# Modulating gathered tokens on their way out of PSUM, a projection in token-tile order, and small tables behind the first expert chunks

## The chip, the cores and the metric

The kernel runs on one core of a Trainium2 chip. The metric is the device time of one execution, in microseconds (us); smaller is better. Of several executions the median is taken.

## The reference, cut to what matters

One layer: a token mixer, a LayerNorm, and a mixture of experts in which each of 256 tokens goes to 4 of 32 experts. `sc2` and `sh2` are rows made from the conditioning vector; what the change touches lies between the mixer's last product and the experts' first.

```python
h = _layer_norm(x) * (1 + sc1) + sh1
y = _token_mixer(h, ...)              # ends with  m @ w_out + b_out
x = _layer_norm(ALPHA * x + g1 * y, post1_g, post1_b)
h = _layer_norm(x) * (1 + sc2) + sh2  # "second modulation"
logits = h @ w_router + b_router      # 256 x 32
top_logits, top_idx = lax.top_k(logits, 4)
top_w = jax.nn.softmax(top_logits)
for each expert e, over its tokens:   # 32 experts
    gate, up = split(h[tok] @ w_gu[e] + b_gu[e])     # 1024 x 2048 weights
    act = (min(gate, 7) * sigmoid(1.702 * gate)) * (clip(up, -7, 7) + 1)
    y[tok] += top_w * (act @ w_dn[e] + b_dn[e])      # 1024 x 1024 weights
x = _layer_norm(ALPHA * x + g2 * y, post2_g, post2_b)
```

Everything is float32, D is 1024, and the 256 tokens are two tiles of 128 (t = 0 and 1).

## The kernel before

**The mixer** takes the first 300 us or so. Its products are made of pieces: a float32 operand is split in a high and a low part (ACT casts the high one, DVE subtracts for the low one, L148 for weights, L119 for activations), and three matmuls make one product. Some weight chunks are "native", that is, used unsplit.

**The chain** leads from the mixer to the experts. The projection with `w_out` (L685 to L705) takes four chunks of 1 MB; chunk 0 is native and the other three are split. Its loop goes over pairs of chunks, in each over the two token tiles, and calls `prepare()` and `prepare_router()` in the middle of it. For each tile the LayerNorm follows on DVE (`c_mul` L739, `c_add` L745 and L747, `c_gain` L758, `c_norm` L761; squares and roots on ACT), giving `hn`, the normalised and not yet modulated tokens. `hn` is transposed on PE (L768), multiplied with the router's weights, into which `prepare_router()` has folded the modulation (L778), and `c_top` (L792 on) finds the four experts. In parallel `c_h2` puts the second modulation on `hn` with two POOL operations (L781, L782) and splits the result `h2` for the gather. Ranks of the experts, places of the tokens and one-hot matrices follow. `g2_step` sets single matmuls of another product (`g2`, L493) between all this as filling.

**The gather** (`gather`, `gather_mm` L944) multiplies one-hot matrices with `h2_hi` and `h2_lo` and leaves the tokens of a batch of jobs in columns of a PSUM tile, four groups (kk = 0 to 3) of two 128-row blocks each; ACT copies each group to SBUF (L968).

**The experts' stream**: 30 jobs, the first for expert 0 (its weights can be loaded before the router has run) and 29 for experts chosen by their rank in number of tokens, each with a fixed capacity of 192, 128, 64 or 32 tokens. The first has 64. A job takes 8 chunks of gate/up weights (`gu_mm`, L1095 and L1106) and 4 chunks of down weights (L1237, L1246), 1 MB each, in two rings of 7 and 4 buffers that SP fills (L197, L205). Small pieces of other jobs are "units": lists of steps that `begin()` and `tick()` run one at a time between chunks, from the list `waiting`. Tokens beyond an expert's capacity are taken by tail jobs; the tables that these need and the bias columns of all jobs are made once, after the first gather and before the first chunk (L1003 to L1049), and the combine weights right behind (`c_exp`, `c_comb`, transposes L1325). The four "start units" (L1313) begin the output with the down bias.

**What sets the order.** Each engine works its instructions in the order in which they stand in its queue. DVE's order is as written from L724 to the end; PE's and ACT's is as written till `chain.close()`, and a scheduler's after it. Where the scheduler chooses, as in the mixer, an edit can move instructions that it doesn't name.

## Time and profile before

| | us |
|---|---|
| median of 3 runs | 1285.02 (1281.32 to 1288.55) |
| the profiled execution | 1284.86 |
| its span | 1282.8 |
| PE busy | 1132.3 (88%) |
| DVE busy | 489.0 (38%) |
| ACT busy | 195.0 (15%) |
| POOL busy | 65.2 (5%) |
| moved by DMA | 449.12 MB, mean 350 GB/s |
| PE's granted clock, mean | 0.946 of full |

The span begins with the first instruction and ends with the last; 2.06 us of the execution's time lie outside of it. The busy share is a mean over stages that differ: in the mixer DVE and PE are both full, in the chain no engine is, and in the stream the DMA moves some 415 GB/s for most of the time. All times below are from the start of the span.

### The profile page before, as it was taken

The page shows a single profiled execution, that of the slowest core. Times are in us where ns is not written, and L with a number is a line of the kernel's source. Part 1 is how long each engine was busy: PE and PEld are TensorE (multiplying, and loading weights), DVE is VectorE, ACT ScalarE, POOL GpSimd, SP SyncE. Part 2 cuts the span into 40 slices and gives each one's busy share as a digit, 9 for nine tenths or more (in the row PEclk, how much of TensorE's full clock was granted, in tenths as well). Part 3 has the DMA queues.
Part 4 walks back from the last instruction along what each step waited for, and adds up shares of the span by engine and source line. Part 5 has one row for each costly group of instructions (what it writes and reads, how often), then busy time and mean ns, then how long its engine had stood idle before and what let it go on. Part 6 is the DMA issues. An engine that isn't in the chain of part 4 may idle for free. (4 is left out here: it accounts for less than half of the span.)

```text
span 1282.8 us, 14332 instructions
## 1 busy us (share of the span) xinstructions
PE 1132.3 (88%) x5454; PEld 553.7 (43%) x5454; DVE 489.0 (38%) x921; ACT 195.0 (15%) x316; POOL 65.2 (5%) x189
## 2 busy tenths in 40 slices
PE   1999999997999989999997999899888977998772
PEld 1998898875534324324331343234222321333110
DVE  6799999867411320321321203222121211132113
ACT  1533233443011000100110010011000100010000
POOL 6000000002300001000010010000000000000000
PEclk9999999998899999999998999899889988899676
DMA  9983446775499999899999999999999999999992
GB/s 366 371 319 132 131 135 208 269 272 227 166 403 388 392 368 387 327 393 402 380 417 417 417 416 401 409 416 416 416 417 416 417 418 417 417 416 417 417 413 77
DMA packets 84311, 449.12 MB, mean 350 GB/s; under 512 B 7377, under 2 KB 7417, under 8 KB 51424
## 3 DMA queue, kind: packets, MB, share of 16 engines
q1 hardware_dynamic: 82672, 443.84, 86.7%
q0 software_dynamic: 1552, 4.15, 0.9%
q8 instruction: 50, 0.82, 0.3%
q14 instruction: 37, 0.30, 0.1%
HBM read 446.92 MB, written 1.05 MB: 349 GB/s over the span
## 5 line engine op out<-in xcount | busy, mean ns | idle before, releaser
L1095 PE MATMUL big<-raw,S 128*32 128x512 f32 (+1 forms) x1600 | 280.3, 632 | 35.4 <-DMA raw<-in_w_gu_dram 35.4
L1106 PE MATMUL big<-raw,S 128*128 128x512 f32 x384 | 175.3, 610 | 0.0
L1271 DVE TENSOR_TENSOR ob<-big,g2c 64x512 f32<-64x512 f32 x48 | 33.1, 689 | 362.9 <-PE big L1246 255.2
L1095 PEld LDWEIGHTS big<-raw,S 128*32 128x32 f32 (+1 forms) x1600 | 63.1, 122 | 210.4 <-issue 129.0
L1106 PEld LDWEIGHTS big<-raw,S 128*128 128x128 f32 x384 | 72.9, 195 | 92.7 <-issue 92.4
L517 DVE SCALAR_TENSOR_TENSOR sg<-ya,par,sg 128x256 f32<-128x256 f32 x240 | 100.3, 476 | 0.7
L1246 PE MATMUL big<-raw,aT 128*32 128x512 f32 x512 | 74.9, 699 | 27.0 <-DMA raw<-in_w_dn_dram 25.7
L1237 PE MATMUL big<-raw,aT 128*128 128x512 f32 x192 | 86.9, 600 | 0.0
L427 PE MATMUL big<-hT,raw 128*128 128x256 f32 x384 | 85.5, 379 | 0.0
L1299 PE MATMUL ms<-ob,ohT 128*128 128x512 f32 x144 | 77.0, 647 | 5.2 <-DVE gt L1139 3.2
L1291 DVE TENSOR_TENSOR y<-y,ms 128x512 f32<-128x512 f32 x72 | 49.0, 686 | 80.7 <-PE ms L1299 80.6
L427 PEld LDWEIGHTS big<-hT,raw 128*128 128x128 f32 x384 | 71.8, 190 | 9.6 <-issue 0.5
L1095 PE MATMUL big<-raw,aT 128*64 128x512 f32 x256 | 63.3, 611 | 4.9 <-DMA raw<-in_w_dn_dram 4.9
L148 DVE TENSOR_TENSOR lo<-raw,hi 128x1024 fp32r<-128x1024 f32 x46 | 55.2, 1217 | 5.9 <-ACT hi L147 4.3
L1237 PEld LDWEIGHTS big<-raw,aT 128*128 128x128 f32 x192 | 35.2, 190 | 51.2 <-issue 51.2
L431 PE MATMUL big<-hThi,lo 128*128 128x256 f32 x192 | 55.1, 289 | 0.8 <-DVE lo L148 0.8
L429 PE MATMUL big<-hThi,hi 128*128 128x256 f32 x192 | 55.8, 291 | 0.0
L147 ACT CAST hi<-raw 128x1024 fp32r<-128x1024 f32 x46 | 46.2, 1050 | 59.5 <-DMA raw<-in_w_in_dram 17.8
L430 PE MATMUL big<-hTlo,hi 128*128 128x256 f32 x192 | 55.0, 287 | 0.1
L1129 ACT COPY g<-big 128x512 f32<-128x512 f32 x16 | 9.4, 585 | 299.0 <-PE big L1095 299.0
L1139 DVE TENSOR_TENSOR gt<-ms,bcols 128x256 f32<-128x256 f32 (+1 forms) x46 | 22.6, 492 | 83.7 <-PE ms L1165 83.7
L1165 PE MATMUL ms<-ident,g 128*128 128x128 f32 x224 | 37.1, 296 | 15.7 <-ACT g L1129 7.6
(329 smaller groups left out, 1176.8 us busy)
## 6 DMA issues: line engine op xcount, KB each, us to landing
raw<-in_w_gu_dram SPq DMA_DIRECT2D x240, 1024.0 KB, 16.7
raw<-in_w_dn_dram SPq DMA_DIRECT2D x120, 1024.0 KB, 16.0
raw<-in_w_mod_dram SPq DMA_DIRECT2D x24, 1024.0 KB, 7.5
raw<-in_w_in_dram SPq DMA_DIRECT2D x24, 1024.0 KB, 6.7
raw<-in_w_b_dram SPq DMA_DIRECT2D x4, 1024.0 KB, 4.9
raw<-in_w_a_dram SPq DMA_DIRECT2D x4, 1024.0 KB, 4.9
raw<-in_w_out_dram SPq DMA_DIRECT2D x4, 1024.0 KB, 7.8
x<-in_x_dram SPq DMA_DIRECT2D x1, 1024.0 KB, 8.7
```

Of the source, the lines that this page charges most:

```text
L148: ve.tensor_tensor(c.lo[q], src, f(c.hi[q]), op=ALU.subtract)
L427: pe.matmul(o, lhsT=ck.raw[:, k2 * D + n * P:k2 * D + (n + 1) * P], rhs=af[:, k], start=b0, stop=b1)
L429: pe.matmul(o, lhsT=ck.hi[k2][:, s], rhs=ahi[:, k], start=b0, stop=False)
L430: pe.matmul(o, lhsT=ck.hi[k2][:, s], rhs=alo[:, k], start=False, stop=False)
L431: pe.matmul(o, lhsT=ck.lo[k2][:, s], rhs=ahi[:, k], start=False, stop=b1)
L517: ve.scalar_tensor_tensor(cT[:, n], ya[:, n, t:t + T], bcol(n, t), cT[:, n], op0=ALU.mult, op1=ALU.add)
L1095: pe.matmul(out_[q * n:(q + 1) * n], lhsT=S, rhs=raw[:, w0(q):w0(q) + 512], start=first_, stop=last_)
L1106: pe.matmul(job.ps[h][:, n * 512:(n + 1) * 512], lhsT=S[:, k, 0:P], rhs=raw[:, h * D + n * 512:h * D + (n + 1) * 512], start=f0, stop=f1)
L1237: pe.matmul(job.pd[0][:, n * 512:(n + 1) * 512], lhsT=job.aT[:, k, 0:P], rhs=raw[:, k2 * D + n * 512:k2 * D + (n + 1) * 512], start=f0, st ...
L1246: pe.matmul(job.pd[0][q * 32:(q + 1) * 32, 0:512], lhsT=job.aT[:, k, 0:32], rhs=raw[:, k2 * D + h * 512:k2 * D + (h + 1) * 512], start=ci ...
L1291: ve.tensor_tensor(yy, yy, box[0], op=ALU.add)
L1299: pe.matmul(box[0], lhsT=w()[r, t * P:(t + 1) * P], rhs=o(n)[r], start=i == 0, stop=i == len(parts_) - 1)
```

## The change

Five things are done. (1) The gather takes `hn` in place of `h2`, and the modulation is put on as a group of gathered tokens leaves PSUM, by two ACTIVATE operations on 128x256 with a scale and a bias column (`gather_out`) in place of one copy of 128x512; `h2` and its POOL operations are gone. (2) The projection does both tiles of the native chunk, then the rest of tile 0, then the rest of tile 1, and there by halves of the output (n). (3) The LayerNorm's sums are taken in halves with BN_STATS (`c_sum`, `c_first`), the router's weights are 32 columns wide and not 128, and the filling matmuls are dealt out otherwise (`G2`). (4) The first job's chunk 0 stands behind the first two groups of the gather, and groups 2 and 3 between later chunks. (5) Tail tables, bias columns, combine weights and the `g2` addition become units that run between the first job's chunks.

```diff
-N_RAW, N_HI, N_LO = 5, 9, 5
+N_RAW, N_HI, N_LO = 5, 9, 6
-H2_POOL = True
-G2 = (5, 1, 1, 1, 1, 1, 1)
+G2 = (4, 3, 2, 1, 1)
...
-        wr = rows.tile([P, KC, P], F32, name="wr", tag="row")
-        gp.memset(wr, 0.0)
+        wr = rows.tile([P, KC, E], F32, name="wr", tag="row")
...
+    pairs = [(ci, k2) for ci in range(4) for k2 in range(2)]
+    for t in range(NT):
+        for ci, k2 in pairs[:2]:
+            for n in range(2):
+                out_mm(t, ci, k2, n)
+    prepare()
+    for ci, k2 in pairs[2:]:
+        for n in range(2):
+            out_mm(0, ci, k2, n)
+    prepare_router()
+    for n in range(2):
+        for ci, k2 in pairs[2:]:
+            out_mm(1, ci, k2, n)
...
+    def c_sum(t, n):
+        ns = slice(n * 512, (n + 1) * 512)
+        if n == 0:
+            L[t]["b"] = sm.tile([P, 2, 6], F32, name=nm("cbst"), tag="cbst")
+        ve.tensor_tensor(hn[:, t, ns], yo[t][:, ns], g1[:, ns], op=ALU.mult)
+        ve.tensor_tensor(x1[:, t, ns], hn[:, t, ns], x1[:, t, ns], op=ALU.add)
+        ve.bn_stats(L[t]["b"][:, n], x1[:, t, ns])
+    def c_first(t):
+        mv = L[t]["mv"] = small("mv", 2)
+        ve.bn_aggr(mv, L[t]["b"])
+        L[t]["r", 0] = small("crs", bufs=4)
+        sc.activation(L[t]["r", 0], mv[:, 1:2], AF.Sqrt, bias=eps, scale=1.0)
+        ve.scalar_tensor_tensor(x1[:, t], x1[:, t], mv[:, 0:1], p1[:, 0], op0=ALU.subtract, op1=ALU.mult)
...
-    def c_h2(t, eng0, eng1):
-        eng0.tensor_tensor(h2[:, t], hn[:, t], sc2, op=ALU.mult)
-        eng1.tensor_tensor(h2[:, t], h2[:, t], sh2, op=ALU.add)
-        sc.copy(h2_hi[:, t], h2[:, t])
+    def c_hi(t):
+        sc.copy(hn_hi[:, t], hn[:, t])
...
+    c_second(0)
+    c_sum(1, 0)
+    c_rec(0, 1)
+    c_norm(0)
...
+    c_transpose(0)
+    c_copies(0)
+    c_hi(0)
+    g2_step(G2[0])
+    c_sum(1, 1)
+    c_first(1)
...
+    def gather_out(S, ps, kk, n):
+        for i in range(2):
+            k = kk * 2 + i
+            sc.activation(S[:, k, 0:n], ps[:, i * T:i * T + n], AF.Identity, bias=modc[:, 1, k:k + 1],
+                          scale=modc[:, 0, k:k + 1])
...
-                sc.copy(S[:, kk * 2:kk * 2 + 2, 0:n], box[0].rearrange("p (k s) -> p k s", k=2)[:, :, 0:n])
+                gather_out(S, box[0], kk, n)
...
-            waiting += start_units()
+            waiting += [tail_unit(), bias_unit(0), bias_unit(1), weight_unit(), gate_unit()] + start_units()
+            first_gather = gather(0)
...
+                if j == 0 and k % 2 == 0:
+                    first_gather[k // 2][1]()
+                    if k < KC - 2:
+                        first_gather[k // 2 + 1][0]()
                 tick()
                 gu_mm(job, k, raw)
                 next_gu()
                 begin()
```

`tail_unit`, `bias_unit` and `weight_unit` hold the operations of L1003 to L1049 and of the combine weights, cut into two or three steps each.

Three places show how instructions move. The first is DVE in the chain's LayerNorm, from the point at which the second tile's sums begin. `big_2314` in before and `big_2313` in after are the second tile's projection in PSUM, the first `hn` row writes the first tile's normalised tokens (in after `hn` also takes the product with g1). Before:

```order
L739 TENSOR_TENSOR h_226_2309<-big_2314,g_27_331 128x1024
L755 RECIPROCAL crs_2524<-crs_2524 128x1
L747 SCALAR_TENSOR_TENSOR x_227_2310,s_271_2530<-x_227_2310,crs_2524,pair_2354 128x1024
L748 TENSOR_SCALAR s_271_2530<-s_271_2530 128x1
L745 SCALAR_TENSOR_TENSOR x_227_2310,s_274_2537<-h_226_2309,x_227_2310 128x1024
L748 TENSOR_SCALAR s_274_2537<-s_274_2537 128x1
L755 RECIPROCAL crs_2535<-crs_2535 128x1
L761 TENSOR_SCALAR hn_2512<-x_227_2310,s_271_2530,crs_2535 128x1024
L758 SCALAR_TENSOR_TENSOR x_227_2310<-x_227_2310,s_274_2537,pair_2354 128x1024
```

After, with what each waits for (PE, ACT, DVE itself):

```order
L766 SCALAR_TENSOR_TENSOR x_226_2309,s_269_2529<-x_226_2309,crs_2525,pair_2335 128x1024 [waits DMASW3_49,DVE_49]
L767 TENSOR_SCALAR s_269_2529<-s_269_2529 128x1 [waits DVE_49]
L749 TENSOR_TENSOR hn_2510<-big_2313,g_27_331 128x512 [waits PE_49]
L750 TENSOR_TENSOR x_226_2309<-hn_2510,x_226_2309 128x512 [waits DVE_49]
L751 BN_STATS cbst_2536<-x_226_2309 128x6 [waits DVE_49]
L761 RECIPROCAL crs_2534<-crs_2534 128x1 [waits Activation_49]
L774 TENSOR_SCALAR hn_2510<-x_226_2309,s_269_2529,crs_2534 128x1024 [waits DVE_49]
L749 TENSOR_TENSOR hn_2510<-big_2313,g_27_331 128x512
L750 TENSOR_TENSOR x_226_2309<-hn_2510,x_226_2309 128x512 [waits DVE_49]
```

The first tile's second half of the LayerNorm (L747, now L766) moves ahead of the second tile's first operation, but the first tile's norm (L774) stays behind an operation of the second tile that waits for PE (L749), and of the second tile's two halves only the first one waits.

The second place is PE in the chain, from the end of the projection on; L493 (after: L492) are the filling matmuls, `ms<-ident,hn` the transposes of a tile, `big<-wr` the router. Before:

```order
L493 MATMUL big_2470<-raw_2471,condT 128x512 x4
L493 MATMUL big_2470<-raw_2473,condT 128x512
L768 MATMUL ms_2551<-ident,hn_2512 128x128 x4
L768 MATMUL ms_2556<-ident,hn_2512 128x128 x4
L493 MATMUL big_2470<-raw_2473,condT 128x512
L778 MATMUL big_2528<-wr,h2T_2513 128x128 x8
L493 MATMUL big_2470<-raw_2473,condT 128x512
L768 MATMUL ms_2600<-ident,hn_2512 128x128 x4
```

After:

```order
L781 MATMUL ms_2543<-ident,hn_2510 128x128 x4
L781 MATMUL ms_2548<-ident,hn_2510 128x128 x4
L492 MATMUL big_2468<-raw_2469,condT 128x512 x4
L791 MATMUL big_2542<-wr,h2T_2511 128x32 x8
L492 MATMUL big_2468<-raw_2471,condT 128x512 x3
L781 MATMUL ms_2589<-ident,hn_2510 128x128 x4
L781 MATMUL ms_2594<-ident,hn_2510 128x128 x4
L791 MATMUL big_2542<-wr,h2T_2511 128x32 x8
```

The five filling matmuls ahead of the first tile's transposes are gone from there; four stand behind them, ahead of the router, and three between the router and the second tile.

The third place is PE from the last group of the first gather into the first job; `big_2827` in before and `big_2727` in after are the first job's sums, L1138 in after is L1095 in before, and L1048, L1050, L1067 in after are L1028, L1030, L1044 in before. Before:

```order
L944 MATMUL ms_2742<-oh_2695,h2hi_2510 128x256 x2
L944 MATMUL ms_2742<-oh_2695,h2lo_2511 128x256 x2
L1010 MATMUL ms_2759<-nt__2756,strict 32x128
L1028 MATMUL ms_2777<-jrhs,ones 128x128
L1030 MATMUL ms_2777<-J,posT 128x20 x2
L1044 MATMUL big_2789<-J,bgr 128x51 x16
L1095 MATMUL big_2827<-raw_2484,S_2711 64x512 x3
L1325 MATMUL big_2789<-ident,comb 32x128 x2
```

After:

```order
L948 MATMUL ms_2730<-oh_2687,hnlo_2509 128x256 x2
L1138 MATMUL big_2727<-raw_2482,S_2708 64x512 x4
L1028 MATMUL ms_2749<-nt__2697,strict 32x128
L1138 MATMUL big_2727<-raw_2484,S_2708 64x512 x4
L948 MATMUL ms_2782<-oh_2687,hnhi_2508 128x256 x2
L948 MATMUL ms_2782<-oh_2687,hnlo_2509 128x256 x2
L948 MATMUL ms_2782<-oh_2687,hnhi_2508 128x256 x2
L948 MATMUL ms_2782<-oh_2687,hnlo_2509 128x256 x2
L1048 MATMUL ms_2791<-jrhs,ones 128x128
L1050 MATMUL ms_2791<-J,posT 128x20 x2
L1138 MATMUL big_2727<-raw_2486,S_2708 64x512 x4
L1067 MATMUL ms_2806<-J,bgr 128x51 x8
```

The first chunk stands where the tail tables' first matmul stood, and the tables and bias columns lie between chunks.

## Rows read from the trace of the kernel before

**Rows 1.** Stages: us; busy us (count) PE, PEld, DVE, ACT, POOL; clock; DMA; GB/s.
```profile
343.00:452.00 109.00, 109.00 (x430) 43.08 (x428) 24.58 (x48) 11.95 (x18) 3.10 (x7) 1.00 0.93 376
700.00:900.00 200.00, 190.44 (x782) 75.26 (x784) 45.92 (x90) 19.37 (x32) 5.68 (x16) 0.97 1.01 413
```

**Rows 2.** Waits of PE from 452 us on: us in total, times, longest.
```profile
PE big L1095 <- DMA raw<-in_w_gu_dram: 35.4, 38, 2.2
```

**Rows 3.** DVE timeline: start, us, operation; the last weight split before the projection.
```profile
271.98 1.21 DVE L148 TENSOR_TENSOR lo<-raw,hi 128x1024 fp32r<-128x1024 f32 x1
```

**Rows 4.** DVE timeline in the chain; in brackets idle before it and its releaser.
```profile
295.13 1.23 DVE L739 TENSOR_TENSOR h<-big,g 128x1024 f32<-128x1024 f32 x1 [0.23 <-PE big L703]
...
296.46 1.28 DVE L747 SCALAR_TENSOR_TENSOR x<-x,crs,pair 128x1024 f32<-128x1024 f32 x1
...
297.79 0.15 DVE L748 TENSOR_SCALAR s<-s 128x1 f32<-128x1 f32 x1
...
299.58 0.17 DVE L755 RECIPROCAL crs<-crs 128x1 f32<-128x1 f32 x1 [0.31 <-ACT crs L752]
...
300.71 3.48 DVE L758 SCALAR_TENSOR_TENSOR x<-x,s,pair 128x1024 f32<-128x1024 f32 x1
...
304.29 3.17 DVE L747 SCALAR_TENSOR_TENSOR x<-x,crs,pair 128x1024 f32<-128x1024 f32 x1
...
309.50 0.81 DVE L761 TENSOR_SCALAR hn<-x,s,crs 128x1024 f32<-128x1024 f32 x1
...
316.05 0.19 DVE L792 TENSOR_TENSOR lg<-big,br 128x32 f32<-128x32 f32 x1 [0.27 <-PE big L778]
```

**Rows 5.** POOL timeline in the same stretch: the modulation of the first tile.
```profile
300.74 2.36 POOL L781 TENSOR_TENSOR h<-hn,sc 128x1024 f32<-128x1024 f32 x1 [30.59 <-ACT h L750]
303.18 3.21 POOL L782 TENSOR_TENSOR h<-h,sh 128x1024 f32<-128x1024 f32 x1
```

**Rows 6.** One line's instructions: count, shortest/median/longest in ns, first and last start.
```profile
L317 DVE BATCH_NORM_STATS2 bst<-vt x4: 631/676/678, 122.9 to 126.0; 128x6 f32<-128x512 f32 x4
...
L968 ACT COPY S<-ms x32: 265/585/590, 325.4 to 1167.6; 128x512 f32<-128x512 f32 x28, 128x128 f32<-128x128 f32 x4
...
L1068 ACT ACTIVATE ohT<-ms x19: 383/383/384, 418.2 to 1247.2; 128x256 f32<-128x256 f32 x19
```

**Rows 7.** PE timeline in the chain; a float32 matmul counts as two.
```profile
294.93 4.46 PE L493 MATMUL big<-raw,condT 128*128 128x512 f32 x10
300.74 1.06 PE L768 MATMUL ms<-ident,hn 128*128 128x128 f32 x8 [1.35 <-DVE hn L761]
...
302.50 1.95 PE L778 MATMUL big<-wr,h2T 128*128 128x128 f32 x16
...
310.46 1.94 PE L768 MATMUL ms<-ident,hn 128*128 128x128 f32 x8 [5.15 <-DVE lg L792]
```

**Rows 8.** PE timeline from the first gather into the first job.
```profile
323.66 0.35 PE L944 MATMUL ms<-oh,h2hi 128*128 128x256 f32 x1
...
328.11 0.40 PE L1010 MATMUL ms<-nt__2756,strict 32*32 32x128 f32 x2
330.55 0.46 PE L1028 MATMUL ms<-jrhs,ones 32*128 32x128 f32 x2 [2.04 <-DVE jrhs L1026]
330.85 0.52 PE L1030 MATMUL ms<-J,posT 32*128 32x20 f32 x4
331.21 6.96 PE L1044 MATMUL big<-J,bgr 32*128 32x51 f32 x32
338.10 3.63 PE L1095 MATMUL big<-raw,S 128*64 128x512 f32 x6
...
345.90 1.12 PE L1313 MATMUL ms<-bdn,combT 32*128 32x512 f32 x2
...
352.79 8.80 PE L1095 MATMUL big<-raw,S 128*64 128x512 f32 x40
```

**Rows 9.** The stretch of the bias columns alone, columns as in rows 1.
```profile
331.30:338.10 6.80, 6.80 (x33) 6.70 (x32) 0.67 (x5) 0.00 (x0) 0.86 (x3) 0.50 0.01 5
```

More of the change, by code (lines that the diff above doesn't have):

```diff
@@ L681, in prepare_router @@
         for k in range(KC):
[L682 removed]
+            sc.mul(wr[:, k], wr[:, k], modc[:, 0, k:k + 1])
     yo = [BIG(), BIG()]
[L686 to L705 removed]
@@ new lines, in out_mm @@
+    def out_mm(t, ci, k2, n):
+        ck = chunk(seq["out"] + ci)
+        ts_ = slice(t * P, (t + 1) * P)
+        k = 2 * ci + k2
+        o = yo[t][:, n * 512:(n + 1) * 512]
+        s = slice(n * 512, (n + 1) * 512)
+        b0, b1 = k == 0, k == KC - 1
+        if ck.native:
+            pe.matmul(o, lhsT=sga[:, k, ts_], rhs=ck.raw[:, k2 * D + n * 512:k2 * D + (n + 1) * 512], start=b0, stop=b1)
+        else:
+            pe.matmul(o, lhsT=m_hi[:, k, ts_], rhs=ck.hi[k2][:, s], start=b0, stop=False)
+            pe.matmul(o, lhsT=m_lo[:, k, ts_], rhs=ck.hi[k2][:, s], start=False, stop=False)
+            pe.matmul(o, lhsT=m_hi[:, k, ts_], rhs=ck.lo[k2][:, s], start=False, stop=b1)
@@ L996, in until @@
             begin()
-    waiting += gather(0)
-    flush()
-    cap = const.tile([E, 1], F32, name="cap")
-    ve.scalar_tensor_tensor(capr, place, rank, capr, op0=ALU.is_equal, op1=ALU.mult, accum_out=cap)
-    rem = const.tile([E, 1], F32, name="rem")
-    ve.tensor_tensor(rem, cnt, cap, op=ALU.subtract)
-    nt_ = const.tile([E, 1], F32, name="nt_")
-    ve.tensor_scalar(nt_, rem, 0.0, None, op0=ALU.is_gt)
-    ve.scalar_tensor_tensor(nt_, rem, float(P), nt_, op0=ALU.is_gt, op1=ALU.add)
-    pst = MS()
@@ L1028 @@
-    pe.matmul(pb[:, 0:P], lhsT=ones[:E, :], rhs=rhs, start=True, stop=True)
-    for t in range(NT):
-        pe.matmul(pb[:, P + t * 64:P + t * 64 + NTAIL], lhsT=f(posT)[:, t * P:(t + 1) * P], rhs=J[:, NV:NJOB],
-                  start=True, stop=True)
-    ve.tensor_copy(intq, pb[0:1, NTAIL:2 * NTAIL + 1])
+    cap, rem, nt_, start, endq = (const.tile([E, 1], F32, name=n) for n in ("cap", "rem", "nt_", "start", "endq"))
     base_q = const.tile([P, NTAIL], F32, name="base_q")
-    ve.tensor_copy(base_q, pb[:, 0:NTAIL])
@@ new lines, in bias_unit, with mm, out_ @@
+    def bias_unit(h):
+        box = []
+        def mm():
+            box.append(MS())
+            for c in range(KC):
+                pe.matmul(box[0][:, c * 64:c * 64 + NJOB], lhsT=bgr[:, (h * KC + c) * P:(h * KC + c + 1) * P],
+                          rhs=J[:, 0:NJOB], start=True, stop=True)
+        def out_():
+            ve.tensor_scalar(bcols[:, h * KC:(h + 1) * KC], box[0].rearrange("p (c j) -> p c j", c=KC)[:, :, 0:NJOB],
+                             float(h), None, op0=ALU.add)
+        return [mm, out_]
@@ L1051, with weight_unit, exps, mm @@
+    def weight_unit():
+        box = []
+        def exps():
+            for t in range(NT):
+                c_exp(t)
+        def mm():
+            for t in range(NT):
+                c_comb(t)
+            box.append(MS())
+            for t in range(NT):
+                pe.transpose(box[0][:E, t * P:(t + 1) * P], comb[:, t], ident)
+        def out_():
+            ve.tensor_copy(combT, box[0][:E, 0:T])
+        return [exps, mm, out_]
     bdn = A8([E, D], name="bdn")
@@ L1321, in start_units, with gate_unit @@
         return [unit(t, n) for t in range(NT) for n in range(2)]
-    ve.tensor_tensor(g2c, g2c, pg2, op=ALU.add)
-    for t in range(NT):
-        pe.transpose(pbs[:E, t * P:(t + 1) * P], comb[:, t], ident)
-    ve.tensor_copy(combT, pbs[:E, 0:T])
-    chain.close()
+    def gate_unit():
+        return [lambda: ve.tensor_tensor(g2c, g2c, pg2, op=ALU.add)]
     batch_of = {j: b for b, js in enumerate(BATCHES) for j in js}
@@ L1348 @@
         if job:
-            until(lambda: left[b] == 0)
+            if j:
+                until(lambda: left[b] == 0)
+            else:
+                first_gather[0][0]()
             gu_open(job)
@@ L1358 @@
         if not last:
+            chain.close()
             continue
```

172 lines of the change are left out of this document (70 added, 102 removed).

## The prediction

> **What bounds the kernel now.** I read the stages first, then PE's waits, then the chain row by row. From 343 to 452 us PE is busy all the time and the DMA is below its best (0.93 share, 376 GB/s), so PE is the bound there; from 700 to 900 the DMA moves 413 GB/s at a share of 1.01 and PE has gaps [rows 1]. PE's waits after 452 us are for weights: 35.4 us for gate/up chunks alone [rows 2]. So the stream's later part is bound by the DMA. That doesn't make an earlier start worthless. While PE is the bound, the rings of 11 chunks are full and SP issues a chunk only when PE gives a buffer back; the point at which the DMA takes over hangs on when PE gave these buffers back. A shift of PE between 343 and 452 is thus a shift of the DMA, and passes to the end whole. What sets that shift is the chain before, where no engine is full: projection, LayerNorm, router, ranks, gather, tables, first chunk. I therefore sum along that chain up to the end of job 0's chunks, and hold the rest constant.
>
> **Part by part: the projection.** The sixth low buffer (N_LO) lets one more weight split run early, and the new order puts it on DVE ahead of the steps that make the projection's left operand, while before it stood behind one of them. It costs 1.21 us [rows 3], of which 1.15 is pitch, and it lies on the path since the first native matmul waits for that operand: +1.15. The matmuls are the same in number. Tile by tile, tile 0 is done some 3 us earlier, but the second half of the sums has no wait of its own, and the first half waits for the last matmul of tile 1: putting the halves of the output apart buys nothing. The second tile is complete at 295.13 before [rows 4], at 296.3 after.
>
> **The LayerNorm.** Before, hn of tile 1 starts at 309.50 and is done at 310.31, 15.2 us after the tile was complete. In it L758 takes 3.48 and L747 3.17, where the same L747 took 1.28 for tile 0 [rows 4]; while they are slow, POOL runs the two modulation operations, 2.36 and 3.21 [rows 5]. These 4.1 us are what the removal of h2 gives back. After, DVE goes through: half a sum of tile 1, three operations at 0.6 (half of the 1.23 of L739 in [rows 4]; BN_STATS takes 0.676 [rows 6]), 1.8; root and norm of tile 0, 1.0; the other half, 1.8; aggregation, 0.2; first gain, 1.3; reciprocal, gain and sum, 1.5 (the 1.28 at 296.46 and the small ones around it, done at 297.8); from there to the next reciprocal, 1.8 (297.79 to 299.58, the square on ACT); norm, 1.0. Together 10.4, so hn of tile 1 is there at 306.7, 3.6 earlier. Tile 0's hn waits in DVE's queue behind tile 1's first half; its lead is lost, and it comes at 299.1 in place of 300.6.
>
> PE is then what is late. Behind the first tile's transposes (0.93 pitch) come four filling steps (4.46 for five, [rows 7], so 3.5), the router (1.85) and three more (2.6). Tile 1's transposes so start at 307.9, not at 306.7. From transposes to the end of the router tile 0 took 300.74 to 304.45; tile 1 took 5.6, from 310.46 to 316.05, its transposes 1.94 against 1.06 [rows 7]: half of the granted clock, after PE had been idle for 5.15. In the new order PE has work right up to the second tile, so I take 3.7. The top-4 of tile 1 starts at 307.9 + 3.7 = 311.6 before any loss of clock, against 316.05 [rows 4]: 4.4 gained. From there to the first gather, 323.66 [rows 8], nothing changes (7.6): 319.2.
>
> The Trainium skill, "TensorE: Matmul & The Clock Gate", Part 1, has the slow clock as the default which activity lifts; by it the gap that the new order leaves on PE speaks against the change (rival A2 has its price). The trace agrees for the second tile of before; no row shows the clock behind the new gap.
>
> **First gather to end of job 0.** Before, 14.4 us lie between the first gather (323.66) and the first expert matmul (338.10): gathers till 328.1, 2.0 waiting for the tables, tables, and bias columns 6.96 at half the clock, 32 matmuls at 0.217 [rows 8, 9]. Job 0's 64 matmuls end, with the four start units between them, at 352.79 + 32/40 of 8.8 = 359.8. After, counted from the first gather: two groups and the way out of the first, 2.4 (four groups take 4.4); 64 matmuls at 0.22, 14.1; the other two groups, 1.9; tables, 0.4 + 0.8 (L1010, L1028 with L1030); bias columns 4.2 at full clock (L1030 has 0.13 each) to 6.9; combine weights' transposes, 0.4; start units, 4 at 1.05 (pitch of L1313), 4.2. These are 28.4 to 31.1; with the bias columns half way, 29.8. Nothing of the work is gone: what is gained is the wait for tables, the low clock and the gaps between small matmuls. Added are waits of PE for evictions between chunks, 0 to 2 us, since each step of a unit has a chunk (0.88) or more to become ready in; I take 1.0. Job 0 ends at 319.2 + 30.8 = 350.0, 9.8 before 359.8.
>
> What is queued behind the new waits: the first chunk waits for the first eviction alone; behind it on PE stands all of job 0. Bias columns wait for DVE's J and a PSUM buffer that the third group's eviction frees; the fourth group, behind the bias columns, waits for them. On SP, tile buffers come free by the projection's end and then by chunks, so the supply moves with PE; the rings hold 11 of job 0's 12 chunks ahead.
>
> **Costs I set near nothing.** Evictions become two of 0.383 in place of one of 0.585 [rows 6], +0.18 for each of 28 groups of 512, at most 5 us if each stood on PE's path; ACT is busy 11.95 of 109 us in the PE-bound stage [rows 1], groups are spread between chunks, and half of them lie in the DMA-bound part. I take 0.4 (bounds 0 and 5). Router matmuls of 32 columns in place of 128 can only help, by at most 0.9; in the fast case the row's 1.95 for 16 is bound by loads, and I take 0. The removed memset, br's addition and c_exp's new place are beside longer work.
>
> The Trainium skill, "Perfetto Trace Analysis", Optimizing Scalar/DVE Operations, speaks against cutting the eviction: a fixed cost for each operation, some 0.05 us on PSUM. By it 28 more operations would be 1.5 us of ACT, an estimate; the rows say 5.
>
> **Sum.** +9.8 gained, less 0.4: 1284.86 - 9.4 = 1275.5 us. The profiled execution is 0.16 below the median of the runs, which is nothing beside their spread.
>
> **Rivals.**
> A2, the low clock strikes tile 0. The new order leaves PE without work from about 296.1 to 299.1, where five filling steps stood before [rows 7]. If tile 0's transposes and router then run as tile 1's did behind its idle stretch, 5.6 and not 3.7, the router ends 1.9 later: 1277.4. It is inside the forecast's range; I count it there, as 0.15 of its chance.
> B, the low clock comes back in job 0. Before, it held from 331.3 through the bias columns into the first chunk [rows 9], after a chain of small matmuls; the chain before the gather is the same now. Ten us at half the clock cost 5: 1280.5. For it: 32-row matmuls still stand between chunks, and the chain is as thin. Against: chunks follow at once, without the 2.04 wait.
> C, PE waits for ACT and DVE between groups, units and chunks by 5 to 6 us and not 1, since the eviction of a group stands one chunk ahead of its use, and table steps are chains of small DVE operations: 1281.
> D, more is gained: no loss of 1.0, bias columns at full clock, hn earlier: 1269.
> E, slower. PE was busy 6.80 of 6.80 us with the bias columns and its clock was still 0.50 [rows 9]: 32-row work alone doesn't lift it. If chunks that are broken up by such work don't either, all of job 0 and the work between it and job 1 runs at half: 25 us of work cost 25 more, 9.4 gained, so 1300. It decides from 10 us of such work on.
> F, the change doesn't do what it says: the wait for a whole tile eats the LayerNorm's gain, and tables that only moved cost as much between chunks: 1283 to 1285.
>
> **How the numbers follow.** Forecast 0.52, B 0.18, C 0.12, D 0.06, E 0.07, F 0.05. The range reaches from D to B and C with the eviction's upper bound taken in part: 1268.5 to 1283. Below it lies part of D, above it E and F. About 0.5% (6.4 us) is what a measurement here can tell from no change: faster is below 1278.6, which holds the forecast but for its upper edge, D, and a little of B, 0.61; within it B, C, F and that edge, 0.31; slower E and the worst of C, 0.08.
>
> **What would show it.** Right: DVE's L766 and L758 of tile 1 at 1.3 each, with POOL idle; first gather near 319, first expert matmul 2.4 after it, job 0 ended near 350, and from 460 on every chunk earlier by the same 9 to 10 us. Wrong: a first gather after 321 (chain), a granted clock of 0.50 within job 0 (B, E), waits of PE for ACT or DVE there above 3 us (C), or PE waits for weights before 450, by which the shift would be lost on the way.

## The result and the profile after

The changed kernel takes 1269.28 us (median of 4 executions, 1268.65 to 1270.5) against 1285.36 before: a ratio of 0.9879, with a 95% interval of 0.9860 to 0.9899. It is faster by 16.1 us; forecast were 9.4, 1275.5, with a range of 1268.5 to 1283. The measured time lies 0.8 us above the lower end of that range. In a second comparison the ratio was 0.9929 (0.9897 to 0.9960), some 9 us: two of its five executions stood at 1269.5 to 1269.9, like the two that were profiled (1268.86 and 1269.94), and three at 1275.4 to 1278.4.

The stages of after, with PE's whole busy time from the first chunk on (columns as in [rows 1]: us, busy time of PE, PEld, DVE, ACT and POOL, granted clock, DMA share, GB/s):

```profile
321.00:343.00 22.00, 22.00 (x121) 10.73 (x118) 6.20 (x29) 4.62 (x9) 4.16 (x11) 1.00 0.95 387
343.00:452.00 109.00, 108.65 (x461) 43.42 (x463) 30.01 (x59) 13.63 (x23) 3.04 (x7) 1.00 0.92 367
700.00:900.00 200.00, 186.79 (x803) 72.89 (x800) 41.77 (x79) 21.34 (x38) 5.68 (x16) 0.98 1.01 413
```

Where before had PE at half the clock in the tables and the first chunk [rows 9], after has 22 us of PE busy without a gap, at full clock, with the DMA at 387 GB/s. The two later stages are much as in [rows 1].

DVE's timeline of after in the chain (start, us, operation, idle before it and its releaser):

```profile
295.07 0.69 DVE L749 TENSOR_TENSOR hn<-big,g 128x512 f32<-128x512 f32 x1 [3.66 <-PE big L696]
...
300.45 1.28 DVE L758 SCALAR_TENSOR_TENSOR x<-x,mv,pair 128x1024 f32<-128x1024 f32 x1
...
301.84 1.28 DVE L766 SCALAR_TENSOR_TENSOR x<-x,crs,pair 128x1024 f32<-128x1024 f32 x1
...
305.16 0.81 DVE L774 TENSOR_SCALAR hn<-x,s,crs 128x1024 f32<-128x1024 f32 x1
...
310.25 0.19 DVE L803 TENSOR_TENSOR lg<-big,br 128x32 f32<-128x32 f32 x1 [1.71 <-PE big L791]
```

The two long operations of the second tile take 1.28 each, where [rows 4] has 3.48 and 3.17. The second tile begins at 295.07 in place of 295.13, its top-4 at 310.25 in place of 316.05. PE's timeline of after, from the first tile's transposes to the end of job 0:

```profile
298.27 1.06 PE L781 MATMUL ms<-ident,hn 128*128 128x128 f32 x8 [3.24 <-DVE hn L774]
...
306.96 1.04 PE L781 MATMUL ms<-ident,hn 128*128 128x128 f32 x8
...
317.86 0.85 PE L948 MATMUL ms<-oh,hnhi 128*128 128x256 f32 x2
...
320.30 1.94 PE L1138 MATMUL big<-raw,S 128*64 128x512 f32 x8
...
328.14 1.98 PE L1067 MATMUL ms<-J,bgr 32*128 32x51 f32 x16
...
337.17 5.37 PE L1138 MATMUL big<-raw,S 128*64 128x512 f32 x24
342.47 1.12 PE L1356 MATMUL ms<-bdn,combT 32*128 32x512 f32 x2
```

Against [rows 8] the first gather is 5.8 us earlier (317.86, was 323.66), the first expert matmul 17.8 (320.30, was 338.10), and the 32 bias matmuls take 4.0 us, were 6.96. Job 0's chunks end at 342.5; the start units (4.2 us) now stand behind it, before they stood in it, so 346.7 is what compares with 359.9: 13.2 us. To the last job this stays: the first matmul of the wide job (the sixth, 192 tokens) is at 460.4 and was at 473.3, 12.9 earlier, and the last gate/up sums leave PSUM at 1232.9, were 1245.7. The two profiles' spans differ by 15.8 us; the remaining 2.9 lie behind the last gate/up sums: from there to the end are 34.1 us after and 37.1 before.

### The profile page after: what moved, and what is told of

Its sections match the earlier page's. It is cut to its first block, busy times and chain, and to the rows that moved or that the text cites. A ratio compares the mean times of both kernels' runs of the same rounds, so it can differ in the third digit from the quotient of the medians.

```text
span 1267.0 us, 14367 instructions
## 1 busy us (share of the span) xinstructions
PE 1123.8 (89%) x5454; PEld 548.3 (43%) x5454; DVE 484.7 (38%) x926; ACT 205.7 (16%) x344; POOL 55.5 (4%) x185
## 5 line engine op out<-in xcount | busy, mean ns | idle before, releaser
L1138 PE MATMUL big<-raw,S 128*32 128x512 f32 (+1 forms) x1600 | 279.0, 631 | 30.3 <-DMA raw<-in_w_gu_dram 30.3
L1149 PE MATMUL big<-raw,S 128*128 128x512 f32 x384 | 172.2, 602 | 0.0
L1138 PEld LDWEIGHTS big<-raw,S 128*32 128x32 f32 (+1 forms) x1600 | 63.3, 122 | 202.7 <-issue 128.8
L1138 PE MATMUL big<-raw,aT 128*64 128x512 f32 x256 | 65.1, 621 | 4.2 <-DMA raw<-in_w_dn_dram 4.1
L1289 PEld LDWEIGHTS big<-raw,aT 128*32 128x32 f32 x512 | 13.9, 118 | 87.5 <-DMA raw<-in_w_dn_dram 59.3
```

What stands on the lines that cost most here:

```text
L1138: pe.matmul(out_[q * n:(q + 1) * n], lhsT=S, rhs=raw[:, w0(q):w0(q) + 512], start=first_, stop=last_)
L1149: pe.matmul(job.ps[h][:, n * 512:(n + 1) * 512], lhsT=S[:, k, 0:P], rhs=raw[:, h * D + n * 512:h * D + (n + 1) * 512], start=f0, stop=f1)
L1289: pe.matmul(job.pd[0][q * 32:(q + 1) * 32, 0:512], lhsT=job.aT[:, k, 0:32], rhs=raw[:, k2 * D + h * 512:k2 * D + (h + 1) * 512], start=ci ...
```

## The experiments

One table for all. The columns are read from each kernel's PE and DVE timelines: end of the projection (PE's last matmul of it), second tile's hn done, first gather, first expert matmul, end of job 0's chunks (in before, e1 and e2 with the four start units in it), first matmul of the wide job; then median and ratio to before with its interval. The positions are those of one profiled execution, the median is that of all. Each ratio is to executions of before beside it: their median is 1282.31 for e1, e2, e4 and e5, 1283.32 for the changed kernel again, e3, e6 and e11, and 1284.30 for e8, e13, e15 and e16. Medians are compared within such a group only.

| kernel | projection | hn | gather | expert | job 0 | wide | us | ratio |
|---|---|---|---|---|---|---|---|---|
| before | 295.1 | 310.3 | 323.7 | 338.1 | 359.9 | 473.3 | 1285.36 | |
| after | 295.0 | 306.0 | 317.9 | 320.3 | 342.5 | 460.4 | 1269.28 | 0.9879 (0.9860 to 0.9899) |
| after, again | 295.9 | 306.9 | 318.8 | 321.2 | 343.4 | 460.8 | 1275.43 | 0.9929 (0.9897 to 0.9960) |
| e1 modulation only | 294.1 | 305.2 | 316.6 | 332.7 | 354.9 | 468.7 | 1280.32 | 0.9982 (0.9967 to 0.9997) |
| e2 tables first | 295.9 | 306.8 | 318.7 | 335.8 | 355.8 | 470.5 | 1281.25 | 0.9994 (0.9976 to 1.0012) |
| e3 old projection order | 297.4 | 310.5 | 323.9 | 326.4 | 349.1 | 469.1 | 1276.65 | 0.9932 (0.9907 to 0.9957) |
| e4 norm first | 295.3 | 305.3 | 319.5 | 322.1 | 344.3 | 463.8 | 1272.24 | 0.9914 (0.9888 to 0.9941) |
| e5 two PSUM tiles | 295.7 | 303.7 | 315.1 | 317.6 | 339.9 | 461.0 | 1270.14 | 0.9897 (0.9872 to 0.9921) |
| e6 POOL traffic back | 294.8 | 308.5 | 319.6 | 322.0 | 344.2 | 463.7 | 1273.33 | 0.9913 (0.9888 to 0.9937) |
| e8 plain copy | 293.6 | 304.5 | 316.4 | 318.9 | 341.1 | 461.8 | 1273.75 | 0.9934 (0.9910 to 0.9958) |
| e11 ring of six | 298.1 | 309.4 | 323.8 | 326.3 | 350.2 | 474.6 | 1289.92 | 1.0046 (1.0031 to 1.0061) |
| e13 gap filled | 295.4 | 306.4 | 317.4 | 320.0 | 342.2 | 460.6 | 1270.38 | 0.9896 (0.9873 to 0.9920) |
| e15 e5 and filling | 293.9 | 301.9 | 313.3 | 315.8 | 338.0 | 461.9 | 1272.35 | 0.9912 (0.9893 to 0.9932) |
| e16 e13 and filling | 294.8 | 305.7 | 316.8 | 320.1 | 343.0 | 466.6 | 1275.97 | 0.9945 (0.9926 to 0.9965) |

The end of the projection differs between profiles by up to 4.5 us (293.6 to 298.1), from the mixer; for the chain, distances from it are compared and not times.

### Part 1 alone (on the kernel before)

```diff
-        eng0.tensor_tensor(h2[:, t], hn[:, t], sc2, op=ALU.mult)
-        eng1.tensor_tensor(h2[:, t], h2[:, t], sh2, op=ALU.add)
-        sc.copy(h2_hi[:, t], h2[:, t])
+        sc.copy(h2_hi[:, t], hn[:, t])
...
-                sc.copy(S[:, kk * 2:kk * 2 + 2, 0:n], ...)
+                gather_out(S, box[0], kk, n)
```

> The kernel before with part 1 of the change alone: the two POOL operations and h2 are gone, the gather takes hn, and the modulation is put on as gathered tokens leave PSUM. Theory (POOL's traffic slows DVE): L758 and L747 of the second tile take 1.3 us each in place of 3.48 and 3.17, the second tile's hn is there 4.1 us earlier (306.2 and not 310.3), first gather at 319.5 to 320, and the time is 4 us below before, 1281 (if the low clock on PE strikes elsewhere, 1280 to 1283). Rival (DVE is slow there for another reason, or PE's filling work takes the place): L758 and L747 stay above 3 us, or the first gather stays after 322, 1284 to 1286.

DVE's timeline of e1, the second tile's long operations:

```profile
299.70 1.29 DVE L758 SCALAR_TENSOR_TENSOR x<-x,s,pair 128x1024 f32<-128x1024 f32 x1
...
301.09 1.28 DVE L747 SCALAR_TENSOR_TENSOR x<-x,crs,pair 128x1024 f32<-128x1024 f32 x1
```

It is the same code as before at a third of the time; up to here only POOL's two operations are gone. From the projection's end to the first gather there are 22.55 us, 28.57 in before and 22.83 in after: up to the gather, part 1 alone gains as much as the whole change. PE's timeline of e1 behind it:

```profile
324.46 0.76 PE L1033 MATMUL ms<-jrhs,ones 32*128 32x128 f32 x2 [2.35 <-DVE jrhs L1031]
...
325.73 7.04 PE L1049 MATMUL big<-J,bgr 32*128 32x51 f32 x32
332.70 3.68 PE L1100 MATMUL big<-raw,S 128*64 128x512 f32 x6
```

The wait for the tables and the slow bias columns are still there, 16.1 us from the gather to the first expert matmul. Of the 6.0 us gained up to the gather 2.1 are lost again up to the end of job 0 (38.3 us from the gather to there, 36.3 in before), so that 4.0 are left, and the time fell by 2.3, 0.4 to 4.2.

### Tables again ahead of the first job

```diff
-            waiting += [tail_unit(), bias_unit(0), bias_unit(1), weight_unit(), gate_unit()] + start_units()
-            first_gather = gather(0)
+            waiting += gather(0) + [tail_unit(), bias_unit(0), bias_unit(1), weight_unit(), gate_unit()]
+            flush()
+            waiting += start_units()
...
```

> The changed kernel with the whole first gather, the tail tables, the bias columns and the combine weights again ahead of the first expert chunk. Theory (the early start of the first job is worth 7 us and passes to the end whole): first gather at 317.9 as in the changed kernel, first expert matmul 12 to 14 us later at 330 to 332, end of job 0 at 349 to 350 and not 342.5, time 1276. In this theory the granted clock falls to 0.50 in the bias columns again, as in before. Rival (the place of the tables is free, since the rings are full and the DMA bounds the end): 1269 to 1270. Second rival (only the low clock costs, and it doesn't come back): 1272 to 1273.

PE's timeline of e2 and its stretch from 330 to 333:

```profile
326.32 0.46 PE L1048 MATMUL ms<-jrhs,ones 32*128 32x128 f32 x2 [2.12 <-DVE jrhs L1042]
...
326.98 6.11 PE L1067 MATMUL ms<-J,bgr 32*128 32x51 f32 x32
334.98 0.88 PE L1088 MATMUL ms<-ident,comb 128*32 128x128 f32 x2 [1.89 <-DVE ex L822]
335.79 3.15 PE L1138 MATMUL big<-raw,S 128*64 128x512 f32 x8
```

```profile
330.00:333.00 3.00, 3.00 (x15) 2.92 (x14) 0.29 (x1) 0.00 (x0) 0.00 (x0) 0.50 0.00 0
```

The theory's gap and its low clock are back: 17.1 us from the gather to the first expert matmul, 2.4 in after. To the end of job 0 it is 37.1 against 24.7 and 4.2 for the start units, 8.2 more. The time is within the noise of before (0.9976 to 1.0012): nearly the whole gain is gone, more than the 7 us expected. Both rivals fell. Part 1, and parts 4 and 5 together, are thus each needed: part 1 is worth 6 us up to the gather, the early start 8 from there. Each without the other leaves little of the gain in the time, 2.3 us in e1 and 0.8 in e2.

### The projection's order

```diff
-    for t in range(NT):
-        for ci, k2 in pairs[:2]:
...
+    for c2 in range(2):
+        for t in range(NT):
+            for ci in (2 * c2, 2 * c2 + 1):
```

> The changed kernel with the projection's loop in the order of before (pairs of chunks, in each both tiles). Theory (the order by tile and by halves is worth nothing, as part 1 alone gave 22.55 us from the projection's end to the first gather with the old order, and the whole change 22.83): 22.5 to 23.5 us from the projection's end to the first gather, time as the changed kernel within 1 us. Rival (tile 0's lead is worth 1.7 us or more, as DVE has then both tiles' sums to do after the projection): 24.5 to 26 us, time 1.5 to 3 us longer.

The rival was right on DVE: hn of tile 1 is done 13.06 us after the projection, 10.95 in after. The order by tile is worth 2.1 us. That it adds nothing beside part 1 comes from the LayerNorm's new form, whose sums are six operations of some 0.69 for a tile where e1 has two of 1.23: with the old order it costs what the new order gives back (e1, old form and old order: 11.14). The first gather is later still, 26.5 us after the projection (22.8 in after): 1.5 us are added between hn and the gather, where PE's clock was low. PE's timeline and its stretch from 300 to 303:

```profile
302.43 1.94 PE L776 MATMUL ms<-ident,hn 128*128 128x128 f32 x8 [5.00 <-DVE hn L769]
304.16 4.61 PE L492 MATMUL big<-raw,condT 128*128 128x512 f32 x8
```

```profile
300.00:303.00 3.00, 0.57 (x3) 0.60 (x4) 2.90 (x6) 0.89 (x3) 0.00 (x0) 0.50 1.01 374
```

After PE had nothing to do for 5.0 us, transposes and filling ran at 0.50. This is the prediction's rival A2, in another kernel. The time decides nothing here: e3's 1276.65 stands beside 1275.43 of the changed kernel, whose executions spread over 9 us.

### POOL's traffic put back

```diff
     c_hi(0)
+    idle_ = A8([P, NT, D], name="idle")
+    gp.tensor_tensor(idle_[:, 0], hn[:, 0], sc2, op=ALU.mult)
+    gp.tensor_tensor(idle_[:, 0], idle_[:, 0], sh2, op=ALU.add)
```

> The changed kernel with POOL made to do the old modulation's two operations on the first tile all the same, into a buffer that nothing reads. Theory (POOL's traffic slows DVE beside it): the second tile's first gain L758 takes about 3.5 us and its second L766 about 3.2, in place of 1.28 each, the three half-width operations beside them are slowed too, second tile's hn 4 to 6 us later, first gather at 22.8 + 4 to 6 us after the projection's end, time 3 to 5 us longer than the changed kernel. Rival (the LayerNorm's new form is what helps, POOL's operations do no harm): within 1 us of the changed kernel in all of these.

DVE's and POOL's timelines of e6:

```profile
297.78 0.68 DVE L749 TENSOR_TENSOR hn<-big,g 128x512 f32<-128x512 f32 x1
298.50 2.44 DVE L750 TENSOR_TENSOR x<-hn,x 128x512 f32<-128x512 f32 x1
300.98 0.69 DVE L751 BATCH_NORM_STATS2 cbst<-x 128x6 f32<-128x512 f32 x1
...
301.95 2.29 DVE L758 SCALAR_TENSOR_TENSOR x<-x,mv,pair 128x1024 f32<-128x1024 f32 x1
```

```profile
298.05 2.35 POOL L841 TENSOR_TENSOR idle<-hn,sc 128x1024 f32<-128x1024 f32 x1 [29.09 <-DVE hn L774]
300.47 2.68 POOL L842 TENSOR_TENSOR idle<-idle,sh 128x1024 f32<-128x1024 f32 x1
```

In the chain the cause is shown: two POOL operations that nothing waits for make hn of tile 1 2.75 us later (13.70 after the projection, was 10.95) and the first gather 2.0 later. The median doesn't show it: 1273.3 is within the spread of the changed kernel beside it (1269.5 to 1278.4). Size and place are other than I expected: two operations are hit, not four. L750 takes 2.44 (0.69 elsewhere) and L758 2.29 (1.28). BN_STATS, with one operand, runs at its usual 0.69 beside the same traffic, and so does L749, with one operand in PSUM, whose 0.68 overlap it for 0.41; L766 came after it.

When each operation ends says more than how long it takes. L750 ends at 300.94, 0.54 us after POOL's L841 (300.40), and L758 at 304.24, 1.09 after L842 (303.15). In before L758 ends 1.09 after L781 and L747 1.07 after L782 [rows 4, rows 5]. These rows read as if a DVE operation that is hit waits for POOL's to end and then takes most of its usual 0.69 or 1.28: the price would be what is left of POOL's operation, not a factor. No run here varies POOL's length to test that.

The Trainium skill, GPSIMD Engine Reference, section 8, says that POOL shares its SBUF interfaces with DVE and names DVE instructions with two SBUF inputs, or in a 2-port mode, as those that contend. The trace of e6 agrees on the first kind: the hit ones, 2.44 and 2.29, have two large SBUF inputs, L749 and BN_STATS one.

### What lies on the path of a longer lead

Two kernels go after the 3.24 us that PE waits for tile 0's hn. e4 moves the norm of tile 0 ahead of the second tile's sum; e5 gives the second tile two PSUM tiles, so that its first half has a wait of its own (the first tile's transposes then go to the third large PSUM tile, and all of tile 1's matmuls go by halves).

```diff
-    c_sum(1, 0)
     c_rec(0, 1)
     c_norm(0)
+    c_sum(1, 0)
```

> The changed kernel with the first tile's norm on DVE ahead of the second tile's first half sum, so that it doesn't wait behind the last matmul of the projection. Theory (the lead of the first tile was lost in DVE's queue, and PE's 3.24 us of idle time before the first tile's transposes are the price): transposes of tile 0 right after the projection, at 295, second tile's hn at 304.8 and not 306.0, top-4 of tile 1 at 308.1 to 309 and not 310.25, first gather at 316 to 316.5, time 1267. Rival (the second tile's DVE chain is the only bound, PE's idle time costs nothing): 1.1 us from DVE alone, first gather at 316.8, time 1268 or so; or no gain at all, 1269.3.

```diff
-    yo = [BIG(), BIG()]
+    yo = [BIG(), None]
...
+    yo[1] = [MS(), MS()]
+    for n in range(2):
+        for ci, k2 in pairs:
+            out_mm(1, ci, k2, n)
...
```

> The changed kernel with the second tile's projection in two PSUM tiles of 512 columns, each with a wait of its own, so that the first half of the sums can run while PE makes the second half. Theory (one wait for the whole tile made the order by halves worthless): first half of tile 1's sums at 291 to 292, tile 0's hn before 295, transposes of tile 0 right at the end of the projection, tile 1's hn at 303.2, top-4 of tile 1 at 306.5, first gather at 314.1, 3.7 us before the changed kernel's 317.86; time 1265.5. Rival (another resource is late next: PE's filling matmuls, or the low clock after less idle time): first gather at 316 to 318, time 1267.5 to 1269.5.

e4 has its transposes at 295.15 as expected, and hn of tile 1 is done 0.9 us sooner after the projection (10.0, in after 10.9), but the first gather comes later, 24.2 us after it (22.8). The time, 1268.3 to 1273.2 in four executions, doesn't tell it from the changed kernel. PE's timeline and the stretch 309 to 312:

```profile
305.49 1.06 PE L781 MATMUL ms<-ident,hn 128*128 128x128 f32 x8 [1.50 <-DVE lg L803]
306.80 3.46 PE L791 MATMUL big<-wr,h2T 128*128 128x32 f32 x16 [0.24 <-ACT h2T L786]
310.07 3.76 PE L492 MATMUL big<-raw,condT 128*128 128x512 f32 x4
```

```profile
309.00:312.00 3.00, 3.00 (x9) 1.97 (x10) 1.49 (x8) 0.00 (x0) 0.20 (x1) 0.50 0.00 0
```

PE's idle time moved from before the first tile (3.24) to before the second (1.50), and there the clock fell: router 3.46 (1.97 in after), filling 3.76 (1.96). From hn to the gather it is 14.1 us, in after 11.9. Neither theory nor rival had that.

e5 did in the chain what was expected: hn of tile 1 8.0 us after the projection (11.0 in after), first gather 19.4 after it (22.8). One wait for the whole tile was what made the halves worthless. But the ratio to before, 0.9897, is no better than after's first 0.9879. PE's timelines around the start of the wide job, e5 and then after:

```profile
452.58 1.07 PE L1290 MATMUL big<-raw,aT 128*32 128x512 f32 x8 [1.48 <-DMA raw<-in_w_dn_dram]
455.06 1.94 PE L1139 MATMUL big<-raw,S 128*32 128x512 f32 x8 [1.41 <-DMA raw<-in_w_gu_dram]
...
460.96 3.60 PE L1150 MATMUL big<-raw,S 128*128 128x512 f32 x8
```

```profile
453.71 1.07 PE L1289 MATMUL big<-raw,aT 128*32 128x512 f32 x8 [0.69 <-DMA raw<-in_w_dn_dram]
456.20 1.06 PE L1138 MATMUL big<-raw,S 128*32 128x512 f32 x8 [1.42 <-DMA raw<-in_w_gu_dram]
...
460.38 3.60 PE L1149 MATMUL big<-raw,S 128*128 128x512 f32 x8
```

At the third job's last matmul e5 is 2.3 us ahead (436.1 against 438.4). Ahead of the wide job PE waits for weights in both, and the last chunk is only 1.1 us earlier: 1.2 went to the DMA. From that chunk to the wide job e5 takes 5.9 us and after 4.2, and the granted clock from 455 to 460 is 0.50 in e5 (the first row) and 1.00 in after (the second):

```profile
455.00:460.00 5.00, 4.18 (x19) 2.45 (x20) 1.15 (x4) 0.89 (x2) 0.00 (x0) 0.50 1.01 421
455.00:460.00 5.00, 2.72 (x21) 1.64 (x21) 2.44 (x6) 1.08 (x3) 0.00 (x0) 1.00 1.01 421
```

Another 1.7 went to the clock. So two things cap a further lead where the 32-token jobs end. The low clock there is no peculiarity of e5: between 455 and 470 the profiles of e3, e4, e6, e8, e11 and e13 have stretches of five us at 0.50 to 0.72 too, both profiles of after none.

### Filling PE's gaps

e13 sets three filling matmuls ahead of the first tile's transposes. e16 adds to it, and e15 adds to e5, two matmuls without use behind each down chunk before the wide job.

```diff
-G2 = (4, 3, 2, 1, 1)
+G2 = (2, 3, 2, 1, 1)
...
+    g2_step(3)
     c_transpose(0)
```

```diff
             dn_mm(last, ci, raw)
+            if j == 4:
+                ps = MS()
+                for i in range(2):
+                    pe.matmul(ps, lhsT=hn[:, 0, 0:P], rhs=raw[:, i * 512:(i + 1) * 512], start=True, stop=True)
```

> The changed kernel with three of the filling matmuls moved ahead of the first tile's transposes, into the 3.2 us in which PE has nothing to do after the projection. Theory (that gap is where the low clock comes from in the chain: the granted clock was 0.50 to 0.8 between 295 and 306 in the profiles of three other kernels with this gap or a longer one, and 1.00 in the changed kernel's own two profiles, so it strikes some executions; those of 1275 to 1278 among the changed kernel's runs are such): clock 1.00 from the projection to the first gather, 22 us from the projection's end to the first gather (second tile's transposes 0.8 us earlier), time 1268 to 1270 in nearly all executions. Rival (the slow executions come from elsewhere, the gap is free): executions of 1275 to 1278 remain, as many as before.

> As the kernel with the filled gap, and in addition two matmuls without use behind each of the four down chunks of the second 32-token job, where PE waits for weights just before the job of 192 tokens (their result is overwritten unread). Theory (the low clock that follows these waits costs up to 3 us where the wide job begins, and that job is bound by PE, so it passes to the end): granted clock 1.00 from 445 to 470, wide job's first matmul at the same distance from the last chunk before it as in the changed kernel's fast profile (4.2 us), time 1267 to 1270, no execution above 1272. Rival (the low clock there is not what spreads the executions, or more work only delays): as the kernel with the filled gap alone, or longer by 1 us.

> The kernel with the second tile's projection in two PSUM tiles (first gather 3.4 us earlier than the changed kernel, but only 0.4 us of it left at the wide job), with the same useless matmuls ahead of the wide job. Theory (1.8 us of the lost lead went to the low clock at the wide job's start, 1.1 to 1.3 to the DMA, which is the bound there): wide job's last gate/up matmul at 504, clock 1.00 from 445 to 470, time 1267 to 1268. Rival (the DMA takes all of the lead: it is busy from 435 on in either case): time as the changed kernel's fast executions, 1269.5 or more.

e13's chain is as expected: 22.0 us from projection to gather, clock 1.00 all through. Ahead of the wide job its clock is 0.72 (455 to 460), and its profiled execution took 1269.2 all the same. Its executions lie from 1267.0 to 1273.1, three below 1269.3 and three above 1271.5, none at 1275 or more. Three of nine of the changed kernel's were; with six executions this doesn't settle whether the gap is the cause.

e15 and e16 were mis-sized by me: the two useless matmuls behind a down chunk take 1.98 us in PE's timeline of e16, longer than PE's waits there (0.7 and 1.4 in after).

```profile
451.74 1.98 PE L1420 MATMUL ms<-raw,hn 128*128 128x512 f32 x4
...
466.56 3.60 PE L1150 MATMUL big<-raw,S 128*128 128x512 f32 x8
```

The clock stayed at 1.00 there, but the filling itself put PE behind the DMA, and the wide job began at 466.6, 6.0 later than in e13 (0.8 of it at the end of job 0). So they don't tell clock from DMA. They show something else: the wide job's delay of 6.0 arrives at the last gate/up sums as 5.7 (1239.0 against 1233.3) and in the time as 5.6. Where the wide job starts is where the end is set, and that holds for nearly all runs: the profiled execution ends 808.5 to 810.9 us behind the wide job's first matmul in every kernel of the table but before (811.6) and e11 (820.2).

### Size of the rings, and what modulation costs

```diff
-N_G, N_D = 7, 4
+N_G, N_D = 6, 4
```

> The changed kernel with six and not seven buffers for gate/up chunks. Theory (PE hands its lead over to the DMA through the rings: when a stage bound by PE ends, the DMA is ahead by what the rings hold): one chunk of 1 MB less is 2.5 us at 414 GB/s for each hand-over that counts, and there are two, before the wide job with 192 tokens and after it: 2.5 to 5 us longer than the changed kernel, and PE's waits for weights after 440 us larger by as much. Rival (rings are never the limit): within 1 us of the changed kernel.

> The changed kernel with one plain copy for each gathered group in place of the two operations with scale and bias: leaves out the second modulation for the experts' input, so that its time shows what the modulation on the way out of PSUM costs. Theory (hidden beside PE and DMA but for the first group): 0 to 0.5 us shorter than the changed kernel, first expert matmul 0.2 us nearer to the first gather. Rival (28 groups with 0.2 to 0.5 us more each stand on the path): 3 to 8 us shorter.

e8 leaves the scale and bias out:

```diff
-            sc.activation(S[:, k, 0:n], ps[:, i * T:i * T + n], AF.Identity, ...)
+        sc.copy(S[:, kk * 2:kk * 2 + 2, 0:n], ...)
```

e11 is 14.5 us longer than the changed kernel beside it (1275.43). Its profile is of its longest execution, 1294.87. Some 5.9 us stand there at the first gather (projection 3.0 later, and PE's clock low in the chain), the rest in the stream: the wide job 14.3 later than in after, the last sums 25.3 (1258.2). The direction is the theory's, the size isn't: one chunk at two places would have been 5. Nor did PE's waits for weights after 440 us grow as expected: they sum to 63.5 in e11 and 64.5 in after. Between 520 and 600 its DMA share is 0.93, in after 1.01, so the shorter ring costs in later jobs too. How many places count, and by what path, stays open.

e8 has the same 2.44 us from gather to first expert matmul as after, not the 0.2 less that I expected, and 24.69 to the end of job 0 against 24.68. On ACT the modulation costs (after, then e8):

```profile
L955 ACT ACTIVATE S<-ms,modc x64: 395/556/566, 319.5 to 1151.5; 128x256 f32<-128x256 f32 x56, 128x64 f32<-128x64 f32 x8
```

```profile
L953 ACT COPY S<-ms 128x512 f32<-128x512 f32 x8 | 4.7, 586 | 29.4 <-PE ms L948 29.4
```

Two of mostly 0.556 in place of one of 0.586, more than the 0.383 I had taken from another ACTIVATE [rows 6], and still nothing on the path up to there. e8's ratio, 0.9934, is not below after's 0.9879 and 0.9929; its profile has the low clock before the wide job (0.53 from 455 to 460), and its time lies in after's own spread, so what the modulation costs in the later stream the times don't tell.

### The changed kernel again

> The changed kernel itself, beside the others on one chip. In the first profile the stream was 12.9 us earlier than in before from the third job on, and another 2.9 us were won behind the last expert chunk, where nothing was changed. Theory: those 2.9 us are chance of one execution; from the last gate/up copy to the end it takes 34 us as in all other runs and the ratio to before is 0.990 (12 to 13 us). Rival: the end is faster for a reason of the change, and the ratio is 0.987 or 0.988 again with an end of 34 us against 37 in before.

The end took 34.2 us, and 33.9 to 34.8 in all twelve others, e1 with the old end among them. The 37.1 of before is thus most likely chance of that one execution, and of 15.8 us between the first two profiles 12.9 are the change. The ratio, 0.9929, is neither the theory's nor the rival's. The spread of the kernel's own executions, 1269.5 to 1278.4, is wider than the theory had; no profile of the upper ones exists. Between hn and the first gather the low clock costs 1.5 us in e3, 2.3 in e4 and 2.6 in e11 (14.5 us for after's 11.9), and 1.7 before the wide job (e5, e8), which is in the direction of the 6 to 8 us; that it is their cause is open.

## Why the prediction was right in kind and short in size

- **Where the time is decided.** The chain sets PE's start, PE's lead passes the PE-bound stage whole, and the DMA carries it to the end: 13.2 us at job 0's end, 12.9 at the wide job, 12.8 at the last sums. That step held. It is not a law: e5's lead lost 2.9 us at the hand-over.
- **The projection, +1.15, failed.** The extra weight split was taken to lie on the path. It did move: behind the first step of the left operand DVE makes one split (274.14) where before made two (271.98 and 279.08). But that step starts at 265.65, in before at 265.83. DVE has three waits of 1.0 to 1.8 us ahead of it (for ACT's cast and for weights), so the split fitted in without delaying that step. The last of them:

```profile
262.03 3.71 DVE L147 TENSOR_TENSOR lo<-raw,hi 128x1024 fp32r<-128x1024 f32 x3 [1.00 <-ACT hi L146]
```

  The first matmul of the projection is at 267.84 (267.79 before), and the second tile was complete at 295.03, not at 296.3. I had costed a moved instruction without looking for idle time ahead of it: 1.2 us.
- **The LayerNorm held**: 10.9 us after the projection for 10.4, with 1.28 for each long operation. Cause shown by e1 and e6. The sentence that tile 0's lead was lost was half right: the wait stands as forecast (3.24 us of PE's idle time), but the order by tile still saves 2.1 us up to hn (e3), which my sum contained without saying so.
- **Top-4 to gather held**: 7.6 forecast, 7.6 measured; gather to first expert matmul 2.4 and 2.4.
- **Job 0 was over-priced by 1.9.** I took the bias columns half way between the clocks, 5.5, and they took 4.0 at full clock; I took 1.0 for PE's waits between chunks, and there were none; other terms were 0.6 too small. Of the eviction's 0.4 nothing shows up to the end of job 0 (e8).
- These terms, 1.3 up to the gather, 1.9 in job 0 and 0.4, take the 9.4 to 13.0; the stream has 12.9. The other 2.9 between the first two profiles are before's end. The size is judged by the profiles: that the second comparison gives some 9 us, close to the forecast, is chance, since three of its five executions have 6 to 8 us more for a reason that wasn't forecast and isn't known.
- **Rivals.** D (1269) came nearest and had 0.06. B and E, the low clock in job 0, didn't come: it came in e2, where tables stood ahead again. C didn't come. A2 didn't come in the changed kernel's profiles but did in those of e3, e6 and e11, and e11 has the changed kernel's chain. F was right only for the halves of the projection.

## What to carry to other kernels

An engine's slow operation is not always its own: before cutting a 3.5 us operation that takes 1.3 elsewhere, look at what another engine does in the same SBUF at that moment, and move that. Small tables that nothing in the first job needs belong behind its first chunks, where PE has work to wait in; here that was worth 8 us, and the shortened chain 6. And price a gain to the point at which the next bound takes over: the same 3 us ahead of the gather were worth nothing more in e5.
